# One generator for both groups' triangular inverses in a gated DeltaNet, with their 64-sized products in turn

## The chip, the cores and the metric

The kernel runs on one core of one Trainium2 chip. The metric is the time of one execution on the device in microseconds; the median of three runs before the change is 2548.24 us (2547.63 to 2548.34).

## The reference

The program is a trunk of two layers on 256 tokens of width 2048: layer 0 is differential attention and a gated MLP with a causal convolution, layer 1 a gated DeltaNet and another such MLP. The change lies in the DeltaNet, in the part that solves a unit lower triangular system for each head and each chunk of 64 tokens:

```python
low = jnp.where(strict, jnp.einsum('bhncd,bhnkd->bhnck', k_beta, k) * decay, 0.0)
a_mat = low + jnp.eye(CHUNK, dtype=low.dtype)
u = lax.linalg.triangular_solve(a_mat, v_beta, left_side=True, lower=True, unit_diagonal=True)
w = lax.linalg.triangular_solve(a_mat, k_beta * jnp.exp(g_c)[..., None], left_side=True, lower=True, unit_diagonal=True)
...
v_new = u_n - jnp.einsum('bhcd,bhde->bhce', w_n, state)
o = jnp.einsum('bhcd,bhde->bhce', qd_n, state) + jnp.einsum('bhck,bhke->bhce', qk_n, v_new)
```

The kernel works on chunks of 128 tokens instead (two for the 256 tokens) and inverts a 128x128 triangular matrix for each of the 32 value heads and each chunk.

## The kernel before

Almost all of the time goes into projections. `dense` (L113, L114, L116) and `dense_tok` (L160 to L162) split each fp32 weight into a high and a low fp32r part (L86 on ScalarE, L87 on VectorE, four buffers each) and multiply both with activations that are split likewise. These are called the big matmuls below: 128x128 weights against 256 or 512 columns. After each chunk of weights `dense` calls `tick`, which moves every background generator in a list on by one `yield`. The generators issue the small work of the DeltaNet, so it falls between the big matmuls. A scheduler then sets the final order of each engine's instructions, by a model of their times; each engine takes its own in that order.

The DeltaNet's 16 query/key heads are done in four batches of four (`nb`, `hb`), and a batch in two groups of two (`gh`), which are four value heads (`gv`) and, with two chunks each, eight matrices a group (`nm`). While batch b runs its projections, `out` multiplies batch b-1's result with the output weights. For a batch, `keys` makes the decayed products of the keys (tile `lt`) and of queries with keys (`qkt`), and GpSimd picks the four 32x32 diagonal blocks of each matrix. `invert` inverts all the batch's 32x32 blocks on VectorE in some 30 steps and leaves them in two layouts, `ttc` and `tcc`. `levels`, called by `group` (L661), joins these blocks to whole inverses. It goes up in four steps with a `yield` between them, each step a lot of small fp32 matmuls and the copies out of PSUM:

- pp (L615): rows 32s to 32s+31, for s = 0 and 2, into the 32 columns behind them; then `pc` is copied, one half on VectorE (L618) and the other on ScalarE (L619)
- px and py (L624, L626): 32x32 products with pc; then L628 (VectorE) puts py into `Ta` and L630 (ScalarE) px into `TT`
- pq (L634): the first 64-sized product, rows 0 to 63 into columns 64 to 127; L635 (VectorE) copies it into the lower half of `Ta`
- pz (L639): the second 64-sized product, rows 64 to 127 into columns 0 to 63, from that half of `Ta`; L640 (VectorE) puts it into `TT`

There are two `TT` and two `Ta`, one for each group. GpSimd puts the diagonal blocks into both (L609, L611). `group` then waits for the values (`to_tokens`, L648, which transposes them) and multiplies with TT and with lt and qkt (L670), normalises, gates and transposes back (L715). All small products take their PSUM from one pool of four banks (`mp`).

The order around the change comes from the list of generators: `invert` and the two `group`s tick one after the other, so that both groups' lots of one step are issued in the same tick, group 0's first.

Of the kernel before, what the change touches and what calls it, by code (L numbers as in the profile page):

```python
# [8 lines left out]
F32 = mybir.dt.float32  # L9
F32R = mybir.dt.float32r  # L10
AF = mybir.ActivationFunctionType
ALU = mybir.AluOpType
# [4 lines left out]
P = 128  # L17
T = 256
# [8 lines left out]
class Trunk:  # L27
# [36 lines left out]
    def mp(self):  # L64
        return self.mps.tile([P, 512], F32, tag="mp", name="mp")
# [410 lines left out]
    def gdn(self, w_gate, w_in, w_z, w_out, nb, hb, gate_ap, const_ap, conv_col, ng, done):  # L476
# [7 lines left out]
        nc, tc, mp = self.nc, self.tc, self.mp  # L484
# [3 lines left out]
        gv = 2 * gh  # L488
        with tc.tile_pool(name="gd", bufs=1) as gd:
# [8 lines left out]
            TTs, Tas = [], []  # L498
# [5 lines left out]
            quad = [slice(32 * s, 32 * s + 32) for s in range(4)]  # L504
# [91 lines left out]
                nc.vector.transpose(tcc.rearrange("p m c -> p c m"), t.rearrange("p i c -> p c i"))  # L596
                inv += [ttc, tcc]

            def levels(TT, Ta, lts, ttc, tcc, m0):

                nm = 2 * len(lts)
                ms = slice(m0, m0 + nm)
                lview = [lt[:, :T].rearrange("p (t c) -> p t c", t=2) for lt in lts]

                def small(n):
                    return mp()[:, :nm * n].rearrange("p (m c) -> p m c", m=nm)

                for s in (1, 3, 0, 2):
                    nc.gpsimd.tensor_copy(TT[quad[s], :, quad[s]], ttc[quad[s], ms, :])  # L609
                for s in range(2):  # L610
                    nc.gpsimd.tensor_copy(Ta[quad[s], :, quad[s]], tcc[quad[s], ms, :])  # L611
                pp = small(32)
                for m in range(nm):
                    for s in (0, 2):
                        nc.tensor.matmul(pp[quad[s + 1], m, :], lview[m // 2][quad[s], m % 2, quad[s + 1]],  # L615
                                         tcc[quad[s], m0 + m, :], start=True, stop=True)
                pc = gd.tile([P, 2 * gv, 32], F32, tag="pc", name="pc", bufs=2)
                nc.vector.tensor_copy(pc[quad[1]], pp[quad[1]])  # L618
                nc.scalar.copy(pc[quad[3]], pp[quad[3]])  # L619
                yield  # L620
                px, py = small(32), small(32)
                for m in range(nm):
                    for s in (2, 0):
                        nc.tensor.matmul(px[quad[s], m, :], pc[quad[s + 1], m, :], ttc[quad[s + 1], m0 + m, :],  # L624
                                         start=True, stop=True)
                    nc.tensor.matmul(py[quad[1], m, :], TT[quad[1], m, quad[1]], pc[quad[1], m, :],  # L626
                                     start=True, stop=True)
                nc.vector.tensor_scalar(Ta[quad[1], :, quad[0]], py[quad[1]], -1.0, None, ALU.mult)  # L628
                for s in (0, 2):
                    nc.scalar.mul(TT[quad[s], :, quad[s + 1]], px[quad[s]], -1.0)  # L630
                yield
                pq = small(64)
                for m in range(nm):
                    nc.tensor.matmul(pq[64:, m, :], lview[m // 2][:64, m % 2, 64:], Ta[:64, m, :], start=True, stop=True)  # L634
                nc.vector.tensor_copy(Ta[64:], pq[64:])  # L635
                yield
                pz = small(64)
                for m in range(nm):
                    nc.tensor.matmul(pz[:64, m, :], Ta[64:, m, :], TT[64:, m, 64:], start=True, stop=True)  # L639
                nc.vector.tensor_scalar(TT[:64, :, 64:], pz[:64], -1.0, None, ALU.mult)  # L640

            def to_tokens(c, vt, g, ready):
                yield
# [5 lines left out]
                nc.scalar.copy(vt[:, :, g:g + 2, :], p.rearrange("p (t v c) -> p t v c", t=2, v=2))  # L649
                ready.append(g)  # L650

            def group(gi, gr, lqs, inv, vt, ready, zts, acts):

                TT, Ta = TTs[gi % 2], Tas[gi % 2]
                n = 2 * len(gr)
                while len(inv) < 2:
                    yield
                yield
                yield
                sub = lqs[2 * gr[0]:2 * gr[-1] + 2]  # L660
                yield from levels(TT, Ta, [lt for lt, _ in sub], *inv, 4 * gr[0])  # L661
                while len(ready) < len(gr):
                    yield
                yield

                def prod(terms):
                    p = mp().rearrange("p (v c) -> p v c", c=P)
                    for v in range(n):
                        for i, (l, r) in enumerate(terms):
                            nc.tensor.matmul(p[:, v, :], l(v), r[:, v, :], start=i == 0, stop=i == len(terms) - 1)  # L670
# [60 lines left out]
            for b in range(nb):  # L731
                heads = range(b * hb, (b + 1) * hb)
                cc = gd.tile([P, 32, 32], F32, tag="s4", name="Cc", bufs=3)
                nc.gpsimd.memset(cc, 0.0)
                lqs, inv, acts, zts, vts = [], [], [], {}, {}
                groups = [range(i, i + gh) for i in range(0, hb, gh)]
                plan = [("k", i) for i in range(hb)] + [("v", 0)] + [("z", g) for g in range(len(groups))]
                for op, i in plan + [("v", i) for i in range(1, hb)]:
                    if op == "k":
                        hq = heads[i]  # L740
                        c = convs(lin(self.dense(w_in[hq * 2], KD, self.h_acts, wide=False)), (hq, nq + hq))
                        self.spawn(keys(hq, c, cc, 2 * i, lqs))
                        if i == hb - 1:
                            self.spawn(invert(cc, lqs, inv))
                    elif op == "z":
                        gr = groups[i]
                        zt = zts[i] = gd.tile([P, 2, gv, P], F32, tag="vz", name="zt", bufs=4)
# [4 lines left out]
                    else:  # L752
                        gi = i // gh
                        gr = groups[gi]
                        if i == gr[0]:
                            vt = gd.tile([P, 2, gv, P], F32, tag="vz", name="vt", bufs=4)
                            ready = []
                            self.spawn(group(gi, gr, lqs, inv, vt, ready, zts, acts))
# [215 lines left out]
```

## Time and profile before

| | |
|---|---|
| median of three runs | 2548.24 us |
| the profiled execution | 2548.44 us |
| its span, from the first to the last instruction | 2546.4 us |
| TensorE busy | 2536.5 us, 17442 matmul records |
| VectorE busy | 1899.7 us |
| ScalarE busy | 1501.9 us |
| granted TensorE clock | 1.0 |
| the DeltaNet's small work in the trace | from about 1105 to 1830 us |

In the rows of the profile PE is TensorE, PEld its loads of weights, DVE VectorE, ACT ScalarE and POOL GpSimd. A group's row has line, engine, operation, output and inputs, shape and count, then busy us, mean ns of one, and the idle time ahead of it with what ended it. A timeline row has the start in us, the duration in us, and the same names; instructions of one kind in a row are merged, and xN is their count. The duration of a matmul is the time until its result has left, and it is longer than the distance to the next start; a cost in time is therefore read from starts. [...]

### The profile page before, as it was taken

To read this page: it belongs to the slowest core of one execution; us is meant where nothing else is said; L and a number is where in the kernel's file an instruction comes from. 1 tells how busy PE (TensorE), PEld (TensorE's weight loads), DVE (VectorE), ACT (ScalarE), POOL (GpSimd) and SP (SyncE) were. 2 spreads that over 40 slices of the span, in tenths; PEclk is the share of its full clock that TensorE was granted. 3 is DMA by queue.
4 is the path that set the end of the run, shared out by engine and by line. 5 is a ranking of instruction groups with operands and counts; after the bars stand their busy time and mean duration, and the time that the engine had idled before them with its cause. 6 is when DMAs were issued, how large, how long until landed. Compare 5 with 4: busy or idle time off the path is not lost.

```text
span 2546.4 us, 44073 instructions
## 1 busy us (share of the span) xinstructions
PE 2536.5 (100%) x17442; PEld 2363.0 (93%) x17442; DVE 1899.7 (75%) x2787; ACT 1501.9 (59%) x2070; POOL 90.6 (4%) x189
## 2 busy tenths in 40 slices
PE   9999999999999999999999999999999999999999
PEld 8998899999999999999999999999999999999998
DVE  7886677777777655679778788788787777786554
ACT  7666656666666444485664674674566666665343
POOL 0000000000000000010111011021000000000000
PEclk9999999999999999999999999999999999999999
DMA  7566566666666666666455565565466666666775
GB/s 246 174 183 178 169 200 201 202 201 201 200 202 202 200 202 199 198 190 204 153 179 186 159 186 174 169 181 172 159 199 201 202 201 202 201 201 206 209 207 153
DMA packets 137775, 487.33 MB, mean 191 GB/s; under 512 B 15552, under 2 KB 18784, under 8 KB 137568
## 3 DMA queue, kind: packets, MB, share of 16 engines
q1 hardware_dynamic: 137280, 484.16, 61.5%
q8 instruction: 137, 2.24, 0.4%
q14 instruction: 70, 0.57, 0.1%
q10 hardware_dynamic: 288, 0.35, 0.0%
HBM read 482.31 MB, written 2.15 MB: 190 GB/s over the span
## 4 chain that ended last, share of the span: by engine, by line
PE 98%; DMA 1%; DVE 1%; ACT 0%; issue 0%; SPq 0%
PE ps L113 49%; PE ps L114 28%; PE ps L116 7%; PE ps L160 3%; PE ps L161 3%; PE ps L162 3%; PE mp L670 2%; PE mp L269 1%; PE mp L558 1%; PE mp L639 0%; PE mp L634 0%; PE mp L648 0%; PE mp L715 0%; PE mp L407 0%; PE mp L437 0%; PE mp L557 0%
## 5 line engine op out<-in xcount | busy, mean ns | idle before, releaser
L87 DVE TENSOR_TENSOR wlo<-raw,whi 128x1024 fp32r<-128x1024 f32 (+2 forms) x909 | 1103.0, 1215 | 510.8 <-ACT whi L86 502.7
L86 ACT CAST whi<-raw 128x1024 fp32r<-128x1024 f32 (+2 forms) x909 | 944.4, 1040 | 877.0 <-PE ps L113 569.0
L113 PE MATMUL ps<-h,whi 128*128 128x512 f32 (+1 forms) x4304 | 1361.2, 357 | 1.2 <-ACT whi L86 1.2
L114 PE MATMUL ps<-h,wlo 128*128 128x256 f32 x4304 | 1178.4, 274 | 0.7 <-DVE wlo L87 0.7
L113 PEld LDWEIGHTS ps<-h,whi 128*128 128x128 f32 x4304 | 817.4, 190 | 88.1 <-ACT whi L86 1.7
L114 PEld LDWEIGHTS ps<-h,wlo 128*128 128x128 f32 x4304 | 827.1, 192 | 2.7 <-DVE wlo L87 1.5
L113 PE MATMUL ps<-ac,whi 128*128 128x512 f32 x1632 | 535.0, 382 | 0.0
L114 PE MATMUL ps<-ac,wlo 128*128 128x256 f32 x1632 | 444.7, 273 | 0.0
L113 PEld LDWEIGHTS ps<-ac,whi 128*128 128x128 f32 x1632 | 308.4, 189 | 42.9 <-PE ps L113 0.2
L114 PEld LDWEIGHTS ps<-ac,wlo 128*128 128x128 f32 x1632 | 313.3, 192 | 0.1
L116 PE MATMUL ps<-h,whi 128*128 128x256 f32 x1040 | 287.1, 276 | 0.0
L116 PEld LDWEIGHTS ps<-h,whi 128*128 128x128 f32 x1040 | 199.5, 192 | 0.5
L162 PE MATMUL ps<-whi,h 128*128 128x512 f32 x384 | 146.1, 380 | 0.0
L161 PE MATMUL ps<-wlo,h 128*128 128x512 f32 x384 | 146.1, 380 | 0.0
L160 PE MATMUL ps<-whi,h 128*128 128x512 f32 x384 | 146.0, 380 | 0.0
L113 PE MATMUL ps<-oc,whi 128*128 128x256 f32 x512 | 143.1, 280 | 0.0
L250 DVE SCALAR_TENSOR_TENSOR cv<-u,fcols,cv 128x255 f32<-128x255 f32 (+1 forms) x344 | 142.8, 477 | 0.0
L116 PE MATMUL ps<-oc,whi 128*128 128x256 f32 x512 | 141.9, 278 | 0.0
L114 PE MATMUL ps<-oc,wlo 128*128 128x256 f32 x512 | 141.4, 276 | 0.0
L116 PEld LDWEIGHTS ps<-oc,whi 128*128 128x128 f32 x512 | 98.2, 192 | 0.5
L113 PEld LDWEIGHTS ps<-oc,whi 128*128 128x128 f32 x512 | 98.2, 192 | 0.4
L114 PEld LDWEIGHTS ps<-oc,wlo 128*128 128x128 f32 x512 | 98.3, 192 | 0.1
(199 smaller groups left out, 2062.2 us busy)
## 6 DMA issues: line engine op xcount, KB each, us to landing
raw<-w_up SPq DMA_DIRECT2D x344, 512.0 KB, 4.8
raw<-w_down SPq DMA_DIRECT2D x160, 512.0 KB, 4.1
raw<-w_in SPq DMA_DIRECT2D x128, 512.0 KB, 4.7
raw<-w_z SPq DMA_DIRECT2D x64, 512.0 KB, 3.8
raw<-w_out SPq DMA_DIRECT2D x64, 512.0 KB, 4.4
raw<-w_qk SPq DMA_DIRECT2D x63, 512.0 KB, 4.6
raw<-w_v SPq DMA_DIRECT2D x32, 512.0 KB, 3.7
raw<-w_o SPq DMA_DIRECT2D x32, 512.0 KB, 4.5
```

Source lines behind the costliest of these rows:

```text
L86: self.cast = nc.scalar.copy(hi, raw)
L87: nc.vector.tensor_tensor(lo, raw, hi.bitcast(F32), ALU.subtract)
L113: nc.tensor.matmul(ps[:, c, :n], hi[:, k, s], self.turns(a[:, :n // T, :]), start=first, stop=False)
L114: nc.tensor.matmul(ps[:, c, :T], lo[:, k, s], self.turns(a[:, :1, :]), start=False, stop=last and wide)
L116: nc.tensor.matmul(ps[:, c, :T], hi[:, k, s], self.turns(a[:, 1:, :]), start=False, stop=last)
L160: nc.tensor.matmul(ps[:, c, :], ah, wh, start=first, stop=False)
L161: nc.tensor.matmul(ps[:, c, :], ah, wl, start=False, stop=False)
L162: nc.tensor.matmul(ps[:, c, :], al, wh, start=False, stop=last)
L250: nc.vector.scalar_tensor_tensor(out[:, j:], u[:, :T - j], taps[n - 1 - j], out[:, j:], ALU.mult, ALU.add)
L269: last = self.nc.tensor.matmul(out, self.onesr, self.pairs(p[:, j]), start=i + j == 0, stop=i + j == n)
L558: nc.tensor.matmul(p[:, P:384], k[:, :P], r, start=True, stop=True)
L670: nc.tensor.matmul(p[:, v, :], l(v), r[:, v, :], start=i == 0, stop=i == len(terms) - 1)
```

## The change

`levels` becomes a generator of its own, spawned once a batch right behind `invert`, and does each step for both groups (`for g in gs`). The first two steps are otherwise the same. The last two become a loop of three turns: pq of group 0; pz of group 0 in turn with pq of group 1, matrix by matrix; pz of group 1. Between the turns is a `yield`. `group` no longer calls `levels`, but waits until its number is in `done` and its values are there. The matmuls, copies and tiles are as many as before.

```diff
-            def levels(TT, Ta, lts, ttc, tcc, m0):
+            def levels(lqs, inv, gs, done):
+
+                while len(inv) < 2:
+                    yield
+                yield
+                yield
+                ttc, tcc = inv
+                nm = 2 * gv
...
+                pcs = []
+                for g in gs:
...
+                    pp = small(32)
+                    for m in range(nm):
                         for s in (0, 2):
+                            nc.tensor.matmul(pp[quad[s + 1], m, :], left(g, m)[quad[s], quad[s + 1]],
+                                             tcc[quad[s], nm * g + m, :], start=True, stop=True)
...
-                pq = small(64)
-                for m in range(nm):
-                    nc.tensor.matmul(pq[64:, m, :], lview[m // 2][:64, m % 2, 64:], Ta[:64, m, :], start=True, stop=True)
-                nc.vector.tensor_copy(Ta[64:], pq[64:])
-                yield
-                pz = small(64)
-                for m in range(nm):
-                    nc.tensor.matmul(pz[:64, m, :], Ta[64:, m, :], TT[64:, m, 64:], start=True, stop=True)
-                nc.vector.tensor_scalar(TT[:64, :, 64:], pz[:64], -1.0, None, ALU.mult)
+                for g in [*gs, len(gs)]:
+                    up, low = g in gs, g > 0
+                    pq = small(64) if up else None
+                    pz = small(64) if low else None
+                    for m in range(nm):
+                        if low:
+                            nc.tensor.matmul(pz[:64, m, :], Tas[g - 1][64:, m, :], TTs[g - 1][64:, m, 64:],
+                                             start=True, stop=True)
+                        if up:
+                            nc.tensor.matmul(pq[64:, m, :], left(g, m)[:64, 64:], Tas[g][:64, m, :],
+                                             start=True, stop=True)
+                    if up:
+                        nc.vector.tensor_copy(Tas[g][64:], pq[64:])
+                    if low:
+                        nc.vector.tensor_scalar(TTs[g - 1][:64, :, 64:], pz[:64], -1.0, None, ALU.mult)
+                        done.append(g - 1)
+                    yield
...
-            def group(gi, gr, lqs, inv, vt, ready, zts, acts):
+            def group(gi, gr, lqs, done, vt, ready, zts, acts):
...
-                while len(inv) < 2:
+                while gi not in done or len(ready) < len(gr):
                     yield
-                yield
-                yield
                 sub = lqs[2 * gr[0]:2 * gr[-1] + 2]
-                yield from levels(TT, Ta, [lt for lt, _ in sub], *inv, 4 * gr[0])
-                while len(ready) < len(gr):
-                    yield
                 yield
...
                         if i == hb - 1:
                             self.spawn(invert(cc, lqs, inv))
+                            self.spawn(levels(lqs, inv, range(len(groups)), solved))
```

What the scheduler makes of it stands in the order of the instructions. On TensorE, in batch 0, the 64-sized lots stood like this before (mp is the PSUM tile, Ta_10400 and TT_10399 belong to group 0, Ta_10404 and TT_10403 to group 1, lt to one head each; the rows left out are big matmuls):

```order
L113 MATMUL ps_12492<-h_77,whi_12591 128x256
L634 MATMUL mp_12175<-Ta_10400,lt_10711 64x64 x4
L634 MATMUL mp_12175<-Ta_10400,lt_10882 64x64 x4
L114 MATMUL ps_12492<-h_77,wlo_12592 128x256
...
L634 MATMUL mp_12185<-Ta_10404,lt_11053 64x64 x4
L634 MATMUL mp_12185<-Ta_10404,lt_11225 64x64 x4
...
L639 MATMUL mp_12225<-TT_10399,Ta_10400 64x64 x8
L114 MATMUL ps_12492<-h_77,wlo_12640 128x256
L116 MATMUL ps_12492<-h_77,whi_12639 128x256
L639 MATMUL mp_12235<-TT_10403,Ta_10404 64x64 x8
```

And this is the same place after the change, where L653 is pq and L650 is pz; from the second to the third lot some 30 big matmuls are left out, and from the first to the second 26:

```order
L653 MATMUL mp_12175<-Ta_10400,lt_10711 64x64 x4
L653 MATMUL mp_12175<-Ta_10400,lt_10882 64x64 x4
...
L650 MATMUL mp_12216<-TT_10399,Ta_10400 64x64
L653 MATMUL mp_12215<-Ta_10404,lt_11053 64x64
...
L653 MATMUL mp_12215<-Ta_10404,lt_11225 64x64
L114 MATMUL ps_12492<-h_77,wlo_12640 128x256
...
L650 MATMUL mp_12265<-TT_10403,Ta_10404 64x64 x8
L685 MATMUL mp_12276<-vt_11169,TT_10399 128x128 x4
L668 MATMUL mp_12282<-con_10393,cv_12134 128x128 x4
```

Four separate lots have become three; in the middle one L650 and L653 alternate eight times, and the last stands straight in front of group 0's first product with its values (L685, which was L670). The other batches have the same three lots.

The first step on TensorE in batch 0, before, with the transposes of values (L648) between the two groups:

```order
L114 MATMUL ps_12492<-h_77,wlo_12495 128x256
L615 MATMUL mp_11992<-tcc_11924,lt_10711 32x32 x8
L615 MATMUL mp_11992<-tcc_11924,lt_10882 32x32 x8
L648 MATMUL mp_12012<-con_10393,cv_11877 128x128 x4
L615 MATMUL mp_12024<-tcc_11924,lt_11053 32x32 x8
L615 MATMUL mp_12024<-tcc_11924,lt_11225 32x32 x8
L116 MATMUL ps_12492<-h_77,whi_12494 128x256
```

And after it, where L624 is pp and L668 the transposes:

```order
L114 MATMUL ps_12492<-h_77,wlo_12495 128x256
L624 MATMUL mp_11992<-tcc_11924,lt_10711 32x32 x8
L624 MATMUL mp_11992<-tcc_11924,lt_10882 32x32 x8
L624 MATMUL mp_12018<-tcc_11924,lt_11053 32x32 x8
L624 MATMUL mp_12018<-tcc_11924,lt_11225 32x32 x8
L668 MATMUL mp_12038<-con_10393,cv_11877 128x128 x4
L116 MATMUL ps_12492<-h_77,whi_12494 128x256
```

The transposes have moved behind both groups' lots, in all four batches. On VectorE, in batch 2, the copies of pc stood like this before, between a cast of weights (L87) and steps of a convolution (L250):

```order
L283 TENSOR_TENSOR x_76<-ps_16672,x_76 128x512
L618 COPY pc_16351<-mp_16334 32x256
L87 TENSOR_TENSOR wlo_16886<-raw_16884,whi_16885 128x1024
L250 SCALAR_TENSOR_TENSOR cv_16662<-u_16660,cols_81,cv_16662 128x253
L618 COPY pc_16383<-mp_16366 32x256
L250 SCALAR_TENSOR_TENSOR cv_16662<-u_16660,cols_81,cv_16662 128x253
L87 TENSOR_TENSOR wlo_16918<-raw_16916,whi_16917 128x1024
L628 TENSOR_SCALAR Ta_10400<-mp_16417 32x8x32
```

And this way after it (L627 is the copy of pc, L640 the piece of Ta):

```order
L283 TENSOR_TENSOR x_76<-ps_16672,x_76 128x512
L627 COPY pc_16351<-mp_16334 32x256
L627 COPY pc_16377<-mp_16360 32x256
L87 TENSOR_TENSOR wlo_16886<-raw_16884,whi_16885 128x1024
L250 SCALAR_TENSOR_TENSOR cv_16662<-u_16660,cols_81,cv_16662 128x253 x2
L87 TENSOR_TENSOR wlo_16918<-raw_16916,whi_16917 128x1024
L640 TENSOR_SCALAR Ta_10400<-mp_16417 32x8x32
```

The second group's copy has moved ahead of the cast and the first convolution step; what stands ahead of the piece of Ta is the same work as before.

More of the change, by code (lines that the diff above doesn't have):

```diff
@@ new lines, in left @@
+                def left(g, m):
+                    return lqs[gv * g + m // 2][0][:, P * (m % 2):P * (m % 2) + P]
+                pcs = []
+                for g in gs:
+                    ms = slice(nm * g, nm * g + nm)
+                    for s in (1, 3, 0, 2):
+                        nc.gpsimd.tensor_copy(TTs[g][quad[s], :, quad[s]], ttc[quad[s], ms, :])
+                    for s in range(2):
+                        nc.gpsimd.tensor_copy(Tas[g][quad[s], :, quad[s]], tcc[quad[s], ms, :])
+                    pp = small(32)
+                    for m in range(nm):
+                        for s in (0, 2):
+                            nc.tensor.matmul(pp[quad[s + 1], m, :], left(g, m)[quad[s], quad[s + 1]],
+                                             tcc[quad[s], nm * g + m, :], start=True, stop=True)
+                    pc = gd.tile([P, nm, 32], F32, tag="pc", name="pc", bufs=2)
+                    nc.vector.tensor_copy(pc[quad[1]], pp[quad[1]])
+                    nc.scalar.copy(pc[quad[3]], pp[quad[3]])
+                    pcs.append(pc)
@@ new lines, in levels @@
+                yield
+                for g in gs:
+                    TT, Ta, pc = TTs[g], Tas[g], pcs[g]
+                    px, py = small(32), small(32)
+                    for m in range(nm):
+                        for s in (2, 0):
+                            nc.tensor.matmul(px[quad[s], m, :], pc[quad[s + 1], m, :], ttc[quad[s + 1], nm * g + m, :],
+                                             start=True, stop=True)
+                        nc.tensor.matmul(py[quad[1], m, :], TT[quad[1], m, quad[1]], pc[quad[1], m, :],
+                                         start=True, stop=True)
+                    nc.vector.tensor_scalar(Ta[quad[1], :, quad[0]], py[quad[1]], -1.0, None, ALU.mult)
+                    for s in (0, 2):
+                        nc.scalar.mul(TT[quad[s], :, quad[s + 1]], px[quad[s]], -1.0)
@@ L734, in gdn @@
                 nc.gpsimd.memset(cc, 0.0)
-                lqs, inv, acts, zts, vts = [], [], [], {}, {}
+                lqs, inv, solved, acts, zts = [], [], [], [], {}
                 groups = [range(i, i + gh) for i in range(0, hb, gh)]
@@ L757, in gdn @@
                             ready = []
-                            self.spawn(group(gi, gr, lqs, inv, vt, ready, zts, acts))
+                            self.spawn(group(gi, gr, lqs, solved, vt, ready, zts, acts))
                         hq = heads[i]
```

31 lines of the change are left out of this document (5 added, 26 removed).

## The prediction, as it was put on record

> **What bounds the kernel now.** I read the page first: span, engines, chain.
>
> ```profile
> span 2546.4 us, 44073 instructions
> PE 2536.5 (100%) x17442; PEld 2363.0 (93%) x17442; DVE 1899.7 (75%) x2787; ACT 1501.9 (59%) x2070; POOL 90.6 (4%) x189
> ...
> PE 98%; DMA 1%; DVE 1%; ACT 0%; issue 0%; SPq 0%
> ...
> L86 ACT CAST whi<-raw 128x1024 fp32r<-128x1024 f32 (+2 forms) x909 | 944.4, 1040 | 877.0 <-PE ps L113 569.0
> ```
>
> TensorE is the bound, and the chain that ended last is 98% TensorE. The last row says that the weights are not late: the casting engine sits idle 877 us, mostly until TensorE hands a buffer back. So a microsecond of TensorE saved comes off the end, and one lost is added. Next, the waits of TensorE: two of the only five rows.
>
> ```profile
> PE ps L113 <- ACT whi L86: 1.2, 1, 1.2
> PE mp L624 <- ACT pc L619: 0.8, 1, 0.8
> ```
>
> One of them, L624, is in the code that changes. The rest of the gain or loss must come from how densely TensorE's own instructions stand, so I went to the timeline of batch 0. First the 64-sized products (L634, L639), by shape and then as a lot between big matmuls; one fp32 matmul leaves two records.
>
> ```profile
> L639 PE MATMUL mp<-TT,Ta 64*64 64x64 f32 x128 | 9.1, 221 | 0.0
> L634 PE MATMUL mp<-Ta,lt 64*64 64x64 f32 x128 | 9.1, 221 | 0.0
> ```
>
> ```profile
> 1222.73 0.28 PE L113 MATMUL ps<-h,whi 128*128 128x256 f32 x1
> 1222.93 1.14 PE L634 MATMUL mp<-Ta,lt 64*64 64x64 f32 x16
> 1224.01 0.38 PE L114 MATMUL ps<-h,wlo 128*128 128x256 f32 x1
> 1224.22 0.28 PE L116 MATMUL ps<-h,whi 128*128 128x256 f32 x1
> 1224.33 0.28 PE L113 MATMUL ps<-h,whi 128*128 128x256 f32 x1
> ```
>
> Big matmuls start 0.11 us apart (1224.33 - 1224.22). From 1222.73 to 1224.22 are 1.49 us, of which two big ones own 0.22: **one lot costs 1.27 us**. Its 16 records start over 1.14 - 0.22 = 0.92 us (0.92 / 15 = 0.06 apart), the last one owns another 0.06, and the remaining 0.29 us are the price of leaving the big shape and coming back. The shape rows give 9.1 us for eight lots each, 1.14 a lot: all 16 lots of the run are alike.
>
> Then the lots of 32-sized products, which already take tiles in turn:
>
> ```profile
> 1213.79 0.28 PE L114 MATMUL ps<-h,wlo 128*128 128x256 f32 x1
> 1213.99 0.69 PE L615 MATMUL mp<-tcc,lt 32*32 32x32 f32 x32
> 1214.61 0.66 PE L648 MATMUL mp<-con,cv 128*128 128x128 f32 x4
> 1215.20 0.69 PE L615 MATMUL mp<-tcc,lt 32*32 32x32 f32 x32
> 1215.82 0.38 PE L116 MATMUL ps<-h,whi 128*128 128x256 f32 x1
> 1216.04 0.28 PE L113 MATMUL ps<-h,whi 128*128 128x256 f32 x1
> ```
>
> ```profile
> 1218.70 0.22 PE L624 MATMUL mp<-ttc,pc 32*32 32x32 f32 x2
> ...
> 1219.71 0.19 PE L626 MATMUL mp<-pc,TT 32*32 32x32 f32 x1
> 1219.84 0.38 PE L116 MATMUL ps<-h,whi 128*128 128x256 f32 x1
> ```
>
> ```profile
> 1231.70 1.06 PE L670 MATMUL mp<-vt,TT 128*128 128x128 f32 x8
> 1232.60 0.60 PE L648 MATMUL mp<-con,cv 128*128 128x128 f32 x4
> ```
>
> What a record costs by itself: 128 columns 0.90 / 8 = 0.112 us, 64 columns 0.06, so 32 columns about 0.032. But L615 alternates two tiles (rows 0-31 into columns 32-63, rows 64-95 into 96-127), and its 32 records stand (0.69 - 0.19) / 31 = 0.016 apart. The lot of L624 and L626 goes round three tiles, and its 96 records (48 matmuls) stand 1.01 / 95 = 0.0106 apart. 2 x 0.016 and 3 x 0.0106 are both 0.032: different tiles of the array run side by side at no cost, and a round costs what one tile's record does.
>
> **The change, part by part.**
>
> (1) *The in-turn lot.* L639 of group 0 (rows 64-127 into columns 0-63) alternates with L634 of group 1 (rows 0-63 into columns 64-127): disjoint like L615's pair. I take it that 32 records then need 16 rounds of 0.06, 0.92 + 0.01 us, not 2 x 0.92 + 0.06. Bounds: nothing gained (serial) to the whole 0.93 gained; I take the whole, since the two in-turn lots above show it.
>
> (2) *Lots.* Before, four separate 64-lots a batch: 4 x 1.27 = 5.07. After: pq of group 0 alone 1.27; the in-turn lot 1.27 + 0.01; pz of group 1 alone, now straight in front of the 128x128 products of `group`, where the way back is cheaper (a lot followed by L648 makes that 0.66 and not 0.60, +0.06; a big matmul after a lot comes +0.10 late), 1.22. Sum 3.77, **1.30 saved a batch**, of which 0.93 is (1).
>
> (3) *The first level.* Before, L648 stood between the two L615 lots. From 1213.79 to 1216.04 are 2.25 us; less two big matmuls (0.22) and L648's own 4 x 0.11 they are 1.59. After, one lot of 64 records: 0.09 + 63 x 0.016 + 0.12 + 0.06 = 1.28. **0.31 saved a batch.** The px/py lot holds both groups in both programs and stays as it is.
>
> (4) *Batch 2's wait.* There TensorE stood still inside the px/py lot:
>
> ```profile
> 1568.30 0.22 PE L624 MATMUL mp<-ttc,pc 32*32 32x32 f32 x2
> ...
> 1568.81 0.19 PE L626 MATMUL mp<-pc,TT 32*32 32x32 f32 x1
> 1569.80 0.25 PE L624 MATMUL mp<-ttc,pc 32*32 32x32 f32 x4 [0.80 <-ACT pc L619]
> ...
> 1570.50 0.38 PE L116 MATMUL ps<-oc,whi 128*128 128x256 f32 x1
> ...
> 1572.48 1.14 PE L634 MATMUL mp<-Ta,lt 64*64 64x64 f32 x16
> ```
>
> ```profile
> 1566.83 0.42 DVE L618 COPY pc<-mp 32x256 f32<-32x256 f32 x1
> 1567.28 1.23 DVE L87 TENSOR_TENSOR wlo<-raw,whi 128x1024 fp32r<-128x1024 f32 x1
> 1568.42 0.47 DVE L250 SCALAR_TENSOR_TENSOR cv<-u,cols,cv 128x253 f32<-128x253 f32 x1
> 1568.93 0.42 DVE L618 COPY pc<-mp 32x256 f32<-32x256 f32 x1
> 1569.38 0.48 DVE L250 SCALAR_TENSOR_TENSOR cv<-u,cols,cv 128x253 f32<-128x253 f32 x1
> 1569.78 1.22 DVE L87 TENSOR_TENSOR wlo<-raw,whi 128x1024 fp32r<-128x1024 f32 x1
> 1571.03 0.75 DVE L628 TENSOR_SCALAR Ta<-mp 32x256 f32<-32x256 f32 x2
> ```
>
> ```profile
> 1569.38 0.36 ACT L619 COPY pc<-mp 32x256 f32<-32x256 f32 x1 [0.66 <-DVE pc L618]
> ```
>
> The lot takes 1570.50 - 1568.30 = 2.20 us, in batch 0 1219.84 - 1218.70 = 1.14: 1.06 lost. VectorE's second pc copy stood behind a cast (L87) and a convolution step, and ScalarE's half copy waits for VectorE's. In the changed order both copies are next to each other on both engines: VectorE's second would end near 1567.7, ScalarE's (0.36) near 1568.1, ahead of the second half of the lot. What is late next: the same VectorE work still precedes the Ta pieces (L628), ready near 1571.45, while TensorE reaches pq at 1572.48 - 1.06 - 0.31 = 1571.11. So it waits some 0.35 there. Bounds: nothing saved to 1.06 saved; I take **0.7**. The cast that moves one place back is hidden by the lead of the weights (L86's row).
>
> (5) *Nothing else costs.* The matmuls, copies and GpSimd pieces are the same in number. Between the dependent lots of the new order stand 16 to 30 (px/py to pq), 26 (pq to in-turn) and 31 to 36 (to pz) big matmuls, 1.8 to 4.0 us at 0.11, against a copy and at most one cast of 1.2 ahead of it: ```profile
> L635 DVE COPY Ta<-mp 64x512 f32<-64x512 f32 x8 | 5.6, 695 | 4.5 <-PE mp L634 4.5
> ```
>
> Copies of that shape take 0.7 us, so 1.9 with the cast. A wait of some tenths in another batch is possible, batch 3 above all, where px/py moves 4 big matmuls earlier; I leave it at nothing. The two groups' products later are as far apart as before, and the last of them still lies under the output projection of batch 2.
>
> Sum: 4 x (1.30 + 0.31) + 0.7 = 7.1 us. The profiled execution took 2548.4 (span 2546.4 and 2.0 around it), so 2541.3 against itself; the median of the runs is 0.2 lower, which gives **2541.1 us**.
>
> **The rivals.**
>
> *Serial.* The 64x64 tiles do not overlap. For: no row shows 64-sized products in turn. Against: the 32-sized lots do it in twos and threes. Gain less 4 x 0.93: 2541.1 + 3.7 = 2544.8. That is also what "the change does not do what it says" would give, since in (2) and (3) only the fewer trips between shapes remain.
>
> *Weight loads bind.* Every record loads its own weights (PEld x17442 beside PE x17442). Big matmuls show that a load of 128 columns fits into 0.11; if one of 64 columns took half, 0.055, and two tiles had to load one after the other, a round would take 0.11: 16 x 0.05 x 4 = 3.2 less, 2544.3. Against: three loads of 32 columns fit into 0.032, which puts 64 columns at 0.02. The Trainium skill, page "TensorE: Matmul & The Clock Gate", section "Measured speedup vs the span model", measured 3.07 times for four row tiles, so 77% of the ideal. By that, as an estimate, a round would take 0.078 and the time would be 2542.3; the rows here (2 x 0.016 = 0.032) show no such loss for two tiles.
>
> *New waits, slower.* TensorE takes its work in order, and each batch is now a chain of dependent lots, pp, px/py, pq, in-turn, pz. If the copy behind each of the last four links came as late as batch 2's pc did (1569.80 - 1568.81, about 1.0), 15 new waits of 1.0 against 6.4 saved make 2556.8; slower by over 0.2% from about 0.77 us a link. For: one such wait exists, and VectorE is 82% busy in batch 0's stretch:
>
> ```profile
> 1200.00:1300.00 100.00, 100.00 (x954) 95.89 (x954) 81.92 (x133) 69.03 (x104) 16.23 (x29) 1.00 0.51 160
> ```
>
> (length, then TensorE, its loads, VectorE, ScalarE.) Against: the distances in (5).
>
> *Some waits.* One or two links late by a microsecond in two or three batches: 2543 to 2545.
>
> **How the numbers follow.** Forecast 0.72; serial 0.10; weight loads 0.07; some waits 0.06; slower 0.05. Within the forecast, (4) and tenths of new waits give 2540.5 to 2542.5. Serial and weight loads have to be inside the range to leave out no more than 2 in 10: 2540.3 to 2545.0. A measurement of this kernel tells about 0.2% (5.1 us) from no change, so faster means under 2543.1: the forecast and a part of the weight-load case (0.03), 0.75; the same: serial, the rest of the weight loads and some waits, 0.20; slower 0.05.
>
> **What would show it.** In the timeline after, the in-turn lot of 32 records is about 1.15 us long (serial: 2.1; bound by loads: 1.9); the L615 records come as one lot of 64; the px/py lot of batch 2 lasts 1.14, not 2.20, and big matmuls before its pq lot show a gap of some 0.35. Wrong would be: rows of waits of TensorE on copies of pc, Ta or TT adding up to more than a microsecond, or 64-sized records in the in-turn lot 0.06 apart.

## The result, and the profile after

The changed kernel takes **2541.39 us** (median of 8 runs, 2540.73 to 2542.52) against 2548.41 for the kernel before on the same chip (8 runs, 2547.63 to 2549.58): a ratio of 0.9973, 95% interval 0.9963 to 0.9982. 2541.1 was forecast. The profiled execution took 2541.33 us, at a granted clock of 1.0 like the one before.

The page of the changed kernel, first: span, engines, and the chain that ended last by engine.

```profile
span 2539.5 us, 44069 instructions
PE 2530.6 (100%) x17442; PEld 2360.5 (93%) x17442; DVE 1899.7 (75%) x2787; ACT 1506.3 (59%) x2073; POOL 91.2 (4%) x189
...
PE 99%; DMA 1%; DVE 0%; ACT 0%; SPq 0%; issue 0%
```

The span is 6.9 us shorter, TensorE issues the same 17442 matmul records and is still the whole chain. So the gain is in how densely those records stand. Next all waits of TensorE (line waited for: total, times, longest):

```profile
PE mp L269 <- DVE qp L262: 1.5, 1, 1.5
PE mp L938 <- DVE onesr L54: 1.3, 1, 1.3
PE ps L113 <- ACT whi L86: 1.0, 1, 1.0
PE mp L653 <- DVE Ta L640: 0.2, 1, 0.2
PE ps L114 <- DVE wlo L87: 0.2, 1, 0.2
```

The wait on pc (L624 before) is gone. In its place stands L653 on Ta, a smaller one. The other four have no part in the change; L269 (query norms, far from the lots) differs from one profiled execution to the next, 1.2 us before, 1.5 here, none to 2.4 in the runs below, so a difference of a microsecond between two single executions says little.

Now the lots in the timeline of batch 0 (start, length, what). First the level pp, one lot of 64 records:

```profile
1213.88 0.28 PE L114 MATMUL ps<-h,wlo 128*128 128x256 f32 x1
1214.09 1.20 PE L624 MATMUL mp<-tcc,lt 32*32 32x32 f32 x64
1215.22 0.66 PE L668 MATMUL mp<-con,cv 128*128 128x128 f32 x4
1215.63 0.36 PE L116 MATMUL ps<-h,whi 128*128 128x256 f32 x1
1215.82 0.28 PE L113 MATMUL ps<-h,whi 128*128 128x256 f32 x1
```

From the big matmul ahead to the second one behind are 1215.82 - 1213.88 = 1.94 us. Less two big ones (0.22) and L668's own 4 x 0.11 that is 1.28; the two lots cost 1.59.

Then the in-turn lot, pz of group 0 (L650) with pq of group 1 (L653):

```profile
1226.80 0.28 PE L113 MATMUL ps<-h,whi 128*128 128x256 f32 x1
1227.00 0.27 PE L650 MATMUL mp<-TT,Ta 64*64 64x64 f32 x1
1227.01 0.27 PE L653 MATMUL mp<-Ta,lt 64*64 64x64 f32 x1
...
1227.16 0.22 PE L650 MATMUL mp<-TT,Ta 64*64 64x64 f32 x1
1227.17 0.22 PE L653 MATMUL mp<-Ta,lt 64*64 64x64 f32 x1
1227.22 0.22 PE L650 MATMUL mp<-TT,Ta 64*64 64x64 f32 x1
...
1227.93 0.22 PE L653 MATMUL mp<-Ta,lt 64*64 64x64 f32 x1
...
1228.29 0.28 PE L116 MATMUL ps<-h,whi 128*128 128x256 f32 x1
```

Look at the starts, not at the lengths, since the end of a matmul's row is modelled by the profile: L650 and L653 start together, 0.01 us apart, and the next pair comes 0.06 us later (1227.16, 1227.22). The 32 records stand in 1227.93 - 1227.00 = 0.93 us, where one group's 16 alone took 0.92. From 1226.80 to 1228.29 are 1.49, less 0.22: the lot costs 1.27, in all four batches.

The last lot, pz of group 1, straight in front of the products of `group` (L685):

```profile
1231.73 1.14 PE L650 MATMUL mp<-TT,Ta 64*64 64x64 f32 x16
1232.81 1.16 PE L685 MATMUL mp<-vt,TT 128*128 128x128 f32 x8
```

The eight records of L685 took 1.16 us, and 1.06 before, when a big matmul stood in front of them (L670 in the prediction's rows): the way back from the 64-sized shape costs them 0.10 here, as it costs a big matmul.

Batch 2, where the wait was; VectorE below TensorE:

```profile
1564.94 0.22 PE L636 MATMUL mp<-ttc,pc 32*32 32x32 f32 x2
...
1566.08 0.38 PE L116 MATMUL ps<-oc,whi 128*128 128x256 f32 x1
...
1567.85 0.27 PE L116 MATMUL ps<-oc,whi 128*128 128x256 f32 x1
1568.33 1.11 PE L653 MATMUL mp<-Ta,lt 64*64 64x64 f32 x16 [0.20 <-DVE Ta L640]
```

```profile
1566.51 1.22 DVE L87 TENSOR_TENSOR wlo<-raw,whi 128x1024 fp32r<-128x1024 f32 x1
1567.76 0.75 DVE L640 TENSOR_SCALAR Ta<-mp 32x256 f32<-32x256 f32 x2
```

The px/py lot takes 1566.08 - 1564.94 = 1.14, and took 2.20. Behind it pq starts 0.48 after the big matmul in front of it, not 0.20 or 0.21 as at the other lots, since the two Ta pieces come only at 1567.76 on VectorE, behind a cast of weights (L87), and the first of them, group 0's, is done near 1568.1. That is 0.27 lost.

### The profile page after: what moved, and what is told of

It is laid out like the page before. It is cut to its first block, busy times and chain, and to the rows that moved or that the text cites. A ratio compares the mean times of both kernels' runs of the same rounds, so it can differ in the third digit from the quotient of the medians.

```text
span 2539.5 us, 44069 instructions
## 1 busy us (share of the span) xinstructions
PE 2530.6 (100%) x17442; PEld 2360.5 (93%) x17442; DVE 1899.7 (75%) x2787; ACT 1506.3 (59%) x2073; POOL 91.2 (4%) x189
## 4 chain that ended last, share of the span: by engine, by line
PE 99%; DMA 1%; DVE 0%; ACT 0%; SPq 0%; issue 0%
PE ps L113 49%; PE ps L114 28%; PE ps L116 7%; PE ps L161 3%; PE ps L162 3%; PE ps L160 3%; PE mp L685 2%; PE mp L269 1%; PE mp L558 1%; PE mp L650 0%; PE mp L668 0%; PE mp L730 0%; PE mp L407 0%; PE mp L437 0%; PE mp L557 0%; DMA lt<-grow 0%
## 5 line engine op out<-in xcount | busy, mean ns | idle before, releaser
L87 DVE TENSOR_TENSOR wlo<-raw,whi 128x1024 fp32r<-128x1024 f32 (+2 forms) x909 | 1103.5, 1215 | 520.4 <-ACT whi L86 512.5
L113 PE MATMUL ps<-h,whi 128*128 128x512 f32 (+1 forms) x4304 | 1362.4, 358 | 1.0 <-ACT whi L86 1.0
L114 PE MATMUL ps<-h,wlo 128*128 128x256 f32 x4304 | 1179.6, 274 | 0.2 <-DVE wlo L87 0.2
L113 PEld LDWEIGHTS ps<-h,whi 128*128 128x128 f32 x4304 | 820.0, 191 | 87.0 <-ACT whi L86 1.5
L114 PEld LDWEIGHTS ps<-h,wlo 128*128 128x128 f32 x4304 | 828.2, 192 | 1.9 <-DVE wlo L87 0.9
L113 PE MATMUL ps<-ac,whi 128*128 128x512 f32 x1632 | 535.0, 382 | 0.0
L114 PE MATMUL ps<-ac,wlo 128*128 128x256 f32 x1632 | 444.9, 273 | 0.0
L113 PEld LDWEIGHTS ps<-ac,whi 128*128 128x128 f32 x1632 | 309.4, 190 | 42.7 <-PE ps L113 0.2
L114 PEld LDWEIGHTS ps<-ac,wlo 128*128 128x128 f32 x1632 | 313.5, 192 | 0.1
L160 PE MATMUL ps<-whi,h 128*128 128x512 f32 x384 | 146.5, 381 | 0.0
L161 PE MATMUL ps<-wlo,h 128*128 128x512 f32 x384 | 146.2, 381 | 0.0
L250 DVE SCALAR_TENSOR_TENSOR cv<-u,fcols,cv 128x255 f32<-128x255 f32 (+1 forms) x344 | 142.9, 478 | 0.0
L113 PE MATMUL ps<-oc,whi 128*128 128x256 f32 x512 | 142.5, 278 | 0.0
L114 PE MATMUL ps<-oc,wlo 128*128 128x256 f32 x512 | 141.8, 277 | 0.0
L114 PEld LDWEIGHTS ps<-oc,wlo 128*128 128x128 f32 x512 | 98.4, 192 | 0.2
L113 PEld LDWEIGHTS ps<-oc,whi 128*128 128x128 f32 x512 | 98.4, 192 | 0.1
```

Of the source, the lines that this page charges most:

```text
L87: nc.vector.tensor_tensor(lo, raw, hi.bitcast(F32), ALU.subtract)
L113: nc.tensor.matmul(ps[:, c, :n], hi[:, k, s], self.turns(a[:, :n // T, :]), start=first, stop=False)
L114: nc.tensor.matmul(ps[:, c, :T], lo[:, k, s], self.turns(a[:, :1, :]), start=False, stop=last and wide)
L160: nc.tensor.matmul(ps[:, c, :], ah, wh, start=first, stop=False)
L161: nc.tensor.matmul(ps[:, c, :], ah, wl, start=False, stop=False)
L250: nc.vector.scalar_tensor_tensor(out[:, j:], u[:, :T - j], taps[n - 1 - j], out[:, j:], ALU.mult, ALU.add)
```

## The experiments

Each kernel was run beside the kernel before on its chip: 2548.97 us for the order not in turn, group by group, the one bank and the two lots, 2549.09 for the turns of two and four, the four tiles and the six tiles. Where a row is given for one batch, the other three are alike unless said.

### The middle lot not in turn

The middle step makes all of pz, then all of pq; everything else as in the changed kernel.

```diff
-                    for m in range(nm):
-                        if low:
-                            nc.tensor.matmul(pz[:64, m, :], ...)
-                        if up:
-                            nc.tensor.matmul(pq[64:, m, :], ...)
+                    for m in range(nm if low else 0):
+                        nc.tensor.matmul(pz[:64, m, :], ...)
+                    for m in range(nm if up else 0):
+                        nc.tensor.matmul(pq[64:, m, :], ...)
```

> The changed kernel, but in the middle turn all eight pz products of group 0 stand ahead of the eight pq products of group 1; lots, trips and copies stay as they are. Theory (two disjoint 64x64 tiles run side by side only when they alternate): the lot of 32 records grows from 0.93 to about 1.87 us from first to last start, 4 x 0.93 = 3.7 us more than the changed kernel's 2541.4, so about 2545.1. Rival (the gain is only the fewer trips between shapes and batch 2's wait): no difference, 2541.4, and the lot was no longer than before anyway.

Measured: 2545.47 us (2543.74 to 2546.43), ratio 0.9986 (0.9977 to 0.9995), span 2543.7. The timeline of the lot (L649 is pz here, L652 pq):

```profile
1228.08 0.97 PE L649 MATMUL mp<-TT,Ta 64*64 64x64 f32 x13
1228.83 0.27 PE L652 MATMUL mp<-Ta,lt 64*64 64x64 f32 x1
1228.88 0.22 PE L649 MATMUL mp<-TT,Ta 64*64 64x64 f32 x1
...
1229.05 0.92 PE L652 MATMUL mp<-Ta,lt 64*64 64x64 f32 x13
1229.90 0.38 PE L114 MATMUL ps<-h,wlo 128*128 128x256 f32 x1
```

The order alone carries the effect: 1.68 us from first to last record (1229.05 + 0.92 - 0.22 - 1228.08, to a rounding) and not 0.93, so 4 x 0.75 = 3.0 us of the gain come from taking turns. The ratios differ by 0.0013, 3.3 us; the spans by 4.2, of which 0.9 is L269, which waited 2.4 us here. The size was missed by a little: 1.87 would be strictly one after the other. TensorE did not wait for pz to be done: the first record of pq starts at 1228.83, while three of pz have still to start (1228.88 and two more). They work on different tiles, and the later one of the program goes ahead. The scheduler cannot have placed them so: an fp32 matmul leaves two records, and 13 records of pz are six matmuls and a half, so pq started between the two records of one pz matmul. That each engine takes its instructions in the scheduler's order, as the description of the kernel before and the prediction have it, is therefore not quite so for TensorE.

### Group by group: four lots again

pq of both groups in one step and pz of both in the next, no lot in turn; the generator stays one, and so do the joint pp and px/py.

```diff
-                for g in [*gs, len(gs)]:
...
+                for g in gs:
+                    pq = small(64)
+                    for m in range(nm):
+                        nc.tensor.matmul(pq[64:, m, :], ...)
+                    nc.vector.tensor_copy(Tas[g][64:], pq[64:])
+                yield
+                for g in gs:
+                    pz = small(64)
+                    for m in range(nm):
+                        nc.tensor.matmul(pz[:64, m, :], ...)
...
+                yield
```

> One generator for both groups as in the changed kernel, but pq of group 0 and 1 in one step and pz of group 0 and 1 in the next, so that four separate 64-sized lots a batch stand between big matmuls as before the change. Theory: what remains of the gain is the first level in one lot (4 x 0.31 = 1.2 us) and most of batch 2's wait (0.5 to 0.7), so 2548.4 - 1.8 = about 2546.6, and the lots cost 1.27 us each again. Rival (the gain comes from moving the levels out of the groups into one generator): about 2541.4.

Measured: 2546.62 us (2545.99 to 2549.21), ratio 0.9991 (0.9982 to 1.0; by the times alone this is hardly told from no gain), span 2544.3. pz of the two groups in the timeline:

```profile
1226.96 1.14 PE L654 MATMUL mp<-TT,Ta 64*64 64x64 f32 x16
1228.45 1.14 PE L654 MATMUL mp<-TT,Ta 64*64 64x64 f32 x16
```

Two lots, 1.49 apart with two big matmuls between: 1.27 each, as before the change. With the 64-sized lots put back, some 2.4 us of the 7 remain, which were (3) and (4) in the prediction (4 x 0.31 + 0.7 = 1.9). In-turn order and the lot saved are the rest.

### Both products into one PSUM bank

pz and pq of the in-turn lot share one PSUM tile: pz writes its partitions 0 to 63 and pq its 64 to 127, at the same time.

```diff
-                    pq = small(64) if up else None
-                    pz = small(64) if low else None
+                    pq = pz = small(64)
```

> The changed kernel with pq and pz of a turn in one PSUM tile (pq in partitions 64 to 127, pz in 0 to 63 of the same bank), so one tile less. Theory (the L615 lot before also had two row tiles writing one PSUM tile 0.016 us apart): the in-turn lot stays at 0.93 us and the time at 2541.4, give or take 0.5. Rival (the Trainium skill, TensorEngine Tiling (Array Packing), section Gotcha 1: PSUM Pressure, says that different row tiles cannot access the same PSUM bank simultaneously): the pair goes one after the other, about 2545.1.

Measured: 2543.03 us (2542.2 to 2545.38), ratio 0.9978 (0.9969 to 0.9987), span 2540.7. The lot, with L649 for pz and L652 for pq:

```profile
1227.48 0.27 PE L649 MATMUL mp<-TT,Ta 64*64 64x64 f32 x1
1227.49 0.27 PE L652 MATMUL mp<-Ta,lt 64*64 64x64 f32 x1
...
1228.41 0.22 PE L652 MATMUL mp<-Ta,lt 64*64 64x64 f32 x1
```

0.93 us again: the bank does not matter to these two tiles, which write different partitions of it. The Trainium skill, page "TensorEngine Tiling (Array Packing)", section "Gotcha 1: PSUM Pressure", says that row tiles cannot use one PSUM bank at the same time; this lot, whose tiles lie in different rows and columns, shows no such loss. The time, expected within 0.5 of 2541.4, is a miss all the same: 2543.03, and a span 1.2 us longer than that of the changed kernel. Part of this is the first wait for weights (L113, 1.5 us and not 1.0) against a shorter one at L269 (1.0 and not 1.5). New is a wait where `group` transposes the gated values back:

```profile
1439.14 0.30 PE L729 MATMUL mp<-con,zt 128*128 128x128 f32 x1 [0.78 <-DVE zt L718]
```

That the PSUM buffer saved has moved the work there is likely, but not shown.

### Turns of two and of four

The middle step takes K matrices of pz, then K of pq, and so on. K = 1 is the changed kernel and K = 8 the first experiment.

```diff
-                    for m in range(nm):
-                        if low:
+                    for m0 in range(0, nm, K):
+                        for m in range(m0, m0 + K if low else 0):
                             nc.tensor.matmul(pz[:64, m, :], ...)
-                        if up:
+                        for m in range(m0, m0 + K if up else 0):
                             nc.tensor.matmul(pq[64:, m, :], ...)
```

For K = 2:

> The changed kernel, but in the middle turn pz and pq alternate by two matrices, not by one. In the run with pz whole ahead of pq the first pq record started next to the last three pz records, so TensorE starts a later matmul on a free tile past some three waiting records. Theory (it looks past about three records): with turns of two, four records each, the lot is almost as short as with turns of one, 0.95 to 1.05 us, and the time 2541.4 to 2541.9. Rival (TensorE starts matmuls strictly in the order of the program, and the three records were the end of one block only): the two tiles overlap only where blocks meet, some 1.4 us, 2543.3.

For K = 4:

> The same with turns of four matrices, eight records. Theory (it looks past about three records): three places where blocks meet, each of which saves what the single one saved there, 1.87 - 1.68 = 0.19 us, so a lot of about 1.3 us and 4 x 0.37 = 1.5 us more than the changed kernel, 2542.9. Rival (any alternation is enough): 0.93 us and 2541.4.

Measured: K = 2 takes 2542.24 us (2540.26 to 2544.09), ratio 0.9972 (0.9961 to 0.9983); K = 4 2543.23 us (2542.07 to 2544.28), ratio 0.9977 (0.9967 to 0.9986). From first to last record the lot takes 0.93, 0.98, 1.32 and 1.68 us for K = 1, 2, 4 and 8. The head and the tail of the lot for K = 4 (L650 pz, L653 pq):

```profile
1226.91 0.50 PE L650 MATMUL mp<-TT,Ta 64*64 64x64 f32 x5
1227.20 0.27 PE L653 MATMUL mp<-Ta,lt 64*64 64x64 f32 x1
...
1228.00 0.45 PE L653 MATMUL mp<-Ta,lt 64*64 64x64 f32 x5
```

A turn of four matrices has eight records. Five of pz have started when the first of pq goes: again three are passed. With turns of two (four records) that reach nearly covers a whole turn, and little is lost; a TensorE that kept to the order would need about 1.4 us there, by the estimate on record.

### Both pq in one lot, both pz in one lot

If two disjoint tiles are free, the stagger between the groups is not needed: group 1 takes the other half of the columns. pq of group 0 goes to columns 64 to 127 and that of group 1 to columns 0 to 63, pz likewise, so that its copies cross the 64 partitions. Two lots of 32 records are left.

```diff
+                pq = small(64)
+                for m in range(nm):
+                    for g in reversed(gs):
+                        nc.tensor.matmul(pq[64 - 64 * g:128 - 64 * g, m, :], left(g, m)[:64, 64:], Tas[g][:64, m, :], start=True, stop=True)
+                for g in gs:
+                    nc.vector.tensor_copy(Tas[g][64:], pq[64 - 64 * g:128 - 64 * g])
+                yield
+                pz = small(64)
+                for m in range(nm):
+                    for g in reversed(gs):
+                        nc.tensor.matmul(pz[64 * g:64 * g + 64, m, :], Tas[g][64:, m, :], TTs[g][64:, m, 64:], start=True, stop=True)
+                for g in gs:
+                    nc.vector.tensor_scalar(TTs[g][:64, :, 64:], pz[64 * g:64 * g + 64], -1.0, None, ALU.mult)
...
```

> pq of both groups in one lot in turn, group 0 into columns 64 to 127 and group 1 into columns 0 to 63, and pz of both groups in one lot likewise; the copies of group 1 move their data across by 64 partitions. Two 64-sized lots a batch and not three, but the two tiles of a pair share their rows and differ only in columns. Theory (tiles that differ in columns alone also run side by side, as L624 and L626 did for 32): each lot 0.93 us, one lot of 1.27 us less a batch, 2541.4 - 5.1 = 2536.3. Rival (tiles on the same rows take the same path for the moving data and go one after the other): 2 x 0.93 more a batch, 2536.3 + 7.5 = 2543.8.

Measured: **2536.36 us** (2535.12 to 2537.18), ratio 0.9950 (0.9937 to 0.9962), span 2533.9. The lots of pq (L647) and pz (L655):

```profile
1224.05 1.15 PE L647 MATMUL mp<-Ta,lt 64*64 64x64 f32 x32
...
1228.89 1.15 PE L655 MATMUL mp<-TT,Ta 64*64 64x64 f32 x32
```

32 records in 1.15 us, as long as a lot of 16: tiles that share their rows and differ only in columns run side by side too. One more lot of 1.27 a batch, 5.1 us in all, is saved, and the spans differ by 5.6. That the two are so near is in part luck: L269's wait, 1.5 us in the changed kernel, is not there, and other things outside the lots took some of that back (waits of 0.3 at L557 and 0.2 at L161 among them).

### Four tiles for the first level

On top of the last kernel, pp of both groups in turn over four tiles (two of group 0, two of group 1 with its output in another 32 columns).

```diff
-                    pp = small(32)
-                    for m in range(nm):
+                pp = small(32)
+                for m in range(nm):
+                    for g in reversed(gs):
                         for s in (0, 2):
-                            nc.tensor.matmul(pp[quad[s + 1], m, :],
+                            nc.tensor.matmul(pp[quad[s + 1 - g], m, :],
...
-                    nc.vector.tensor_copy(pc[quad[1]], pp[quad[1]])
-                    nc.scalar.copy(pc[quad[3]], pp[quad[3]])
+                    nc.vector.tensor_copy(pc[quad[1]], pp[quad[1 - g]])
+                    nc.scalar.copy(pc[quad[3]], pp[quad[3 - g]])
```

> The kernel with two 64-sized lots, and pp of both groups besides in four tiles (group 0 into columns 32 to 63 and 96 to 127 as before, group 1 into 0 to 31 and 64 to 95; the copies of group 1 move across by 32 partitions). Theory (a round costs what one tile's record does, whatever the number of tiles): 64 records in 16 rounds of 0.032, 0.51 us from first to last start and not 1.01, 4 x 0.5 = 2.0 us less than 2536.4, so 2534.4. Rival (the chip starts at most one record in 0.010 us, as in the lot of three tiles): 0.64 us, 2534.9; or no gain beyond two tiles on the same rows: 2536.4.

Measured: 2540.11 us (2539.93 to 2541.6), ratio 0.9965 (0.9951 to 0.9978), span 2539.7: **a miss**, 3.8 us slower than the kernel it is built on. The two ratios were taken on different chips and their intervals overlap, but each of its runs was slower than each of the other's (2539.93 us or more against 2537.18 or less). The lot itself did nearly what was expected: 0.56 us from first to last record (0.51 expected), 0.75 long in place of 1.20. What came in its place is in TensorE's waits and, for batch 0, in VectorE's timeline:

```profile
PE ps L113 <- ACT whi L86: 2.2, 1, 2.2
PE ps L161 <- DVE wlo L87: 2.1, 2, 1.3
PE mp L639 <- ACT pc L631: 1.6, 2, 1.1
...
PE mp L688 <- ACT vt L700: 0.8, 1, 0.8
PE ps L160 <- ACT whi L86: 0.6, 1, 0.6
```

```profile
1218.37 0.42 DVE L630 COPY pc<-mp 32x256 f32<-32x256 f32 x1
1218.82 1.55 DVE L250 SCALAR_TENSOR_TENSOR cv<-u,cols,cv 128x254 f32<-128x254 f32 x3
1220.40 0.41 DVE L630 COPY pc<-mp 32x256 f32<-32x256 f32 x1
```

The scheduler put three convolution steps (L250) between the two copies of pc. ScalarE's half copy waits for the second one, and the px/py lot (L639) for that, 1.1 us in its middle. This is the mechanism of the batch 2 wait, and of the slower rival, back again in a kernel whose edit shortened TensorE's part. Besides, weights came late between 1280 and 1290 us (L161 and L160, 2.7 us together; 0.2 in the kernel with two lots) and a copy of values once (L688, 0.8). Why they did is not shown. The first wait for weights (L113, within the first 10 us) is 1.0 longer than in the kernel with two lots, and L269's wait of 1.1 has no counterpart in that one. These two differ between other runs as well, so some 2 of the 5.8 us between the profiled spans say nothing about the edit.

### Six tiles for the second level as well

px and py of both groups also in one round, in six tiles.

```diff
+                px, py = small(32), small(32)
+                for m in range(nm):
+                    for g in reversed(gs):
                         for s in (2, 0):
-                            nc.tensor.matmul(px[quad[s], m, :], pc[quad[s + 1], m, :], ...)
-                        nc.tensor.matmul(py[quad[1], m, :], TT[quad[1], m, quad[1]], ...)
+                            nc.tensor.matmul(px[quad[s + g], m, :], pcs[g][quad[s + 1], m, :], ...)
+                        nc.tensor.matmul(py[quad[2 + g], m, :], TTs[g][quad[1], m, quad[1]], ...)
```

> That kernel with px and py of both groups in six tiles besides. Theory: 96 records in 16 rounds; six starts 0.0065 us apart (the distance of two tiles in L615's lot) are 0.039 and no longer fit into the 0.032 of a record, so a round takes about 0.039 and the lot 0.63 us and not 1.02: 4 x 0.39 = 1.6 less, 2532.8. Rival 1 (the round stays at 0.032): 0.51 us, 2532.4. Rival 2 (the lot now needs the pc of both groups from its first matmul on, and waits for the later one): a wait of 0.4 us or more a batch takes the gain back, 2534.4 or more.

Measured: **2534.48 us** (2533.32 to 2535.76), ratio 0.9941 (0.9929 to 0.9954), span 2531.5: the lowest time of all, though its interval overlaps that of the two lots (0.9937 to 0.9962). The pp lot, and the ends of the px/py lot:

```profile
1213.33 0.75 PE L625 MATMUL mp<-tcc,lt 32*32 32x32 f32 x64
...
1219.53 0.22 PE L638 MATMUL mp<-ttc,pc 32*32 32x32 f32 x2 [0.39 <-ACT pc L631]
...
1220.36 0.19 PE L640 MATMUL mp<-pc,TT 32*32 32x32 f32 x1
```

The 96 records stand in 1220.36 - 1219.53 = 0.83 us: less than the 1.01 of three tiles, more than the 0.63 expected, and 0.83 in the other batches too. The time is the one that rival 2 named, but by another way: the lot itself is longer than expected, and a wait for pc came in one batch only. The late weights and the long pc wait of the four-tile kernel are not there; only 0.39 us of it, in batch 0. As the pp lot is the same in both kernels, four tiles alone do not bring those waits; that the order of the work around them did is argued, not shown.

## Why the prediction was right

The time came within 0.3 us, and the terms hold one by one, each to 0.2 or better. That they sum to within 0.3 is in part luck: two terms came out smaller and one larger, and runs of the same kernel differ by more (2540.73 to 2542.52). What the trace gives for each, in us of span:

| term | predicted | in the trace after |
|---|---|---|
| (1), (2) lots of 64, 4 batches | 4 x 1.30 = 5.20 | 4 x 1.25 = 5.00 |
| (3) first level, 4 batches | 4 x 0.31 = 1.24 | 1.24 |
| (4) batch 2 | 0.70 | 1.06 - 0.27 = 0.79 |
| (5) others | 0 | -0.11 |
| sum | 7.1 | 6.9 |

Outside the lots, L269's wait grew by 0.3, and the start of the run with its first waits for weights (L113, L114) came out 0.2 shorter. That makes 6.8, where the spans differ by 6.9.

**(1) right.** 0.93 us from first to last record was predicted and measured. Both rivals against it fall: serial by this lot, and more strictly by the first experiment, where the same records in another order need 1.68; weight loads by the same 0.93, since a round of 0.11 would have made 1.8. The Trainium skill, page "TensorE: Matmul & The Clock Gate", section "Measured speedup vs the span model", has 3.07 times for four row tiles, 77% of the ideal, which by the prediction's estimate would have made 16 x 0.078 = 1.2; no such loss shows here for two tiles. Four tiles, two on each of two sets of rows, reach some 91% in the pp lot of the last two kernels (0.56 us for 64 records from first to last, against 16 x 0.032 = 0.51).

**(2) right but for one size.** The lot ahead of L685 was priced at 1.22, from a cheap way back seen at L648 (+0.06). It cost 1.27: L685's eight records took 1.16 and not 1.06. That is the 0.05 a batch between 1.30 and 1.25.

**(3) right.** 1.28 predicted, 1.28 measured, in one lot of 64 as said.

**(4) right in its mechanism.** Both copies of pc came in time, and the wait went on to Ta, at pq, for the reason given. It was 0.27 and not 0.35; only the size was off, by a tenth.

**(5) nearly.** One loss of the kind held possible came, in batch 3, the batch that was named. Its px/py lot in the timeline:

```profile
1756.72 0.22 PE L636 MATMUL mp<-ttc,pc 32*32 32x32 f32 x2
...
1757.23 0.19 PE L638 MATMUL mp<-pc,TT 32*32 32x32 f32 x1
1757.34 0.22 PE L636 MATMUL mp<-ttc,pc 32*32 32x32 f32 x2
```

Between the groups is a gap of 0.11 us. No row names what it waited for; both copies of pc had ended more than 0.7 us earlier, so the reason given for batch 3 is not the one, and the cause stays open.

**The slower rival** did not come true here, but its mechanism is real: the four-tile kernel lost 1.6 us to copies of pc that came late (L639), and with the late weights and values more than it had gained. Whether such a copy is late is set by where the scheduler puts it, and for the changed kernel its order told that ahead of the run.

## What to carry to other kernels

Where TensorE is the bound and small products stand in lots between big ones, count lots before records: a trip to the small shape and back cost 0.3 us here, and products on two or three disjoint tiles came free as long as they alternated. Merge lots and let the tiles alternate matrix by matrix; two groups whose dependent steps are alike can share a lot directly with different output columns (2536.36 us), without staggering one behind the other (2541.39 us). After each merge look where the scheduler puts the copies that the next lot needs: one that slipped behind three steps of other work made TensorE wait 1.1 us, nearly the 1.27 of a lot.

## What the hardware did that was not expected

- TensorE does not keep to program order between tiles. A record of a free tile started ahead of up to three earlier records that waited for another tile (turns of 1, 2, 4 and 8 matrices: 0.93, 0.98, 1.32 and 1.68 us for the same 32 records). The Trainium skill, page "TensorE: Matmul & The Clock Gate", Part 3, section "The mechanism", holds that matmuls start and end strictly in order; the starts in the first experiment's rows differ from that, and it is shown here for 64-sized fp32 tiles in different rows and columns.
- Six tiles of 32 do not run six at a time: 96 records took 0.83 us where six tiles at 0.032 a round would need 16 x 0.032 = 0.51, and three tiles needed 1.01. Four tiles came near their ideal (0.56 against 0.51). Four of the six read the same 32 rows, where the pp lot has two on each of its sets of rows; whether that is why six fall behind no run here tells.
- Two tiles in different rows and columns wrote one PSUM bank in turn, in different partitions, at no cost (0.93 us either way).
